# The MLPs of a two-layer decoder step: up and down projections apart, hidden features through DRAM, two token chunks multiplied as 2x2 blocks in seven products (Strassen)

## The chip, the core and the metric

One core of a Trainium2 chip runs the whole program. The metric is the device time of one execution in microseconds (us), lower is better. The engines go by their names in the profile: PE is TensorE's matmul and PEld its weight load, DVE is VectorE, ACT is ScalarE, POOL is GpSimd, and SP issues every DMA of this kernel in one queue, in program order. Each engine runs its own instructions in order and waits on semaphores of the others.

## The reference, cut to what matters

One inference step over 1024 prompt tokens and 8 x 8 sample tokens, 1088 in all, through two layers of width 1024. Layer 0 is a gated mixer, layer 1 a dilated attention; after each of them comes the same kind of MLP, with a hidden width of 4096:

```python
def sq_relu_mlp(x, w_up, w_down):
    h = jnp.square(jax.nn.relu(jnp.einsum('bld,df->blf', x, w_up)))
    return jnp.einsum('blf,fd->bld', h, w_down)
...
xp = layer_norm(ALPHA * xp + mp, ln1_g[layer], ln1_b[layer])
xp = layer_norm(ALPHA * xp + sq_relu_mlp(xp, w_mlp_up[layer], w_mlp_down[layer]), ln2_g[layer], ln2_b[layer])
```

All of it is float32; the new cache rows are outputs too, which for the kernel means 56 copies of up to 1 MB from DRAM to DRAM.

## The kernel before, in words

Activations lie with the features on the 128 partitions and the tokens along a row. `XH` and `XL` hold the layer's input as a high and a low part in float32r (`split`: ACT rounds the high part, DVE or POOL subtracts it), `ACC` holds the sum that is being built up, all three with 8 blocks of 1088 tokens. The tokens are cut into three chunks (`TC`), of 384, 384 and 320 in some order.

A float32 product is three matmuls on float32r parts, high x high, high x low and low x high (`group`), summed in one PSUM bank; there are 8 banks (`ps`). A weight piece (`raw`, 1024 numbers on a partition, two buffers) comes from DRAM on the SP queue and is converted into high and low parts (`convert`: ACT, then POOL) in one of six `wp` buffers. `pump` converts the next piece after a matmul group while fewer than `cap` (6 here) are converted and not released.

`mlp` goes through the hidden width in eight blocks of 512 (`ff`). In a block, `up` makes the 512 hidden features of every chunk: 24 matmuls a group (8 feature blocks x 3), then ACT takes relu from PSUM into `t`, DVE multiplies it onto PSUM, ACT writes the high part into the scratch tile `h` and DVE the low part. `down` multiplies them by the block's rows of the down weights, 12 matmuls a group, and DVE adds the group onto `ACC` from PSUM. Nothing of the hidden features leaves the core. Of the 56 cache copies one is issued (`shift`) after each weight piece of layer 0's MLP.

The order in which work of several streams is emitted comes from a model of the engines (`Model`, `Driver`). All operations pass through a recorder, so that every row of the profile has its line, L188, and rows are told apart by their tiles.

## Time and profile before

| | |
|---|---|
| median of 3 runs | 2763.81 us (2763.4 to 2763.81) |
| span of the profiled execution | 2761.2 us |
| PE busy | 2695.0 us, 98% of the span |
| DVE, ACT, POOL busy | 1058.6, 761.3, 626.8 us |
| moved by the DMA queue SP issues to | 220.20 MB, 25.0% of 16 engines' span |

The span runs from the first to the last instruction of one profiled execution; the times of the runs are 2.2 to 2.6 us longer than this span. A busy share is an average over stages; the two MLPs are two of them, from about 340 to 1105 us and from about 1950 to 2707 us.

### The profile page before, as it was taken

How to read it: one execution, taken by the hardware profiler on the slowest of the kernel's cores; microseconds unless marked ns; L12 is line 12 of the kernel's file. 1: busy time of each engine (PE TensorE's matmuls, PEld its weight loads, DVE VectorE, ACT ScalarE, POOL GpSimd, SP SyncE). 2: the span in 40 equal slices, each digit the busy share in tenths (PEclk: the TensorE clock that was granted, in tenths of full speed). 3: DMA queues.
4: the chain of work that ended last, by engine and by line, in shares of the span. 5: the costliest groups of instructions: out<-in, count | busy, mean ns of one | idle time of the engine just before them, and what ended most of it. 6: DMA issues, size and time to landing. Idle time of an engine off the chain costs nothing.

```text
span 2761.2 us, 42360 instructions
## 1 busy us (share of the span) xinstructions
PE 2695.0 (98%) x17783; PEld 2596.4 (94%) x17783; DVE 1058.6 (38%) x2422; ACT 761.3 (28%) x1531; POOL 626.8 (23%) x357
## 2 busy tenths in 40 slices
PE   9999999999999999899999999998899999999997
PEld 8999999999999999888888888887799999999997
DVE  4306472222222223843434434447922222222226
ACT  4213152221122112432333333333432212211221
POOL 1421243221222222311211211214542112122212
PEclk9999999999999999999999999999999999999999
DMA  4111112333333342033332332331111111111111
GB/s 151 44 52 32 46 39 96 114 117 133 137 137 117 133 156 103 27 100 111 100 116 81 94 113 78 105 97 40 46 54 46 39 46 47 46 40 46 51 35 66
DMA packets 271901, 222.92 MB, mean 81 GB/s; under 512 B 9519, under 2 KB 262651, under 8 KB 270813
## 3 DMA queue, kind: packets, MB, share of 16 engines
q1 hardware_dynamic: 271708, 220.20, 25.0%
q8 instruction: 140, 2.29, 0.3%
q14 instruction: 53, 0.43, 0.0%
HBM read 207.94 MB, written 65.97 MB: 99 GB/s over the span
## 4 chain that ended last, share of the span: by engine, by line
PE 87%; DVE 6%; issue 2%; POOL 1%; ACT 0%; POOLq 0%; DVEq 0%; ACTq 0%
PE ps L188 87%; DVE ACC L188 2%; DVE t L188 1%; DVE h L188 1%; POOL ACC L188 1%; DVE wp L188 1%; DVE XL L188 0%; POOL t L188 0%; ACT t L188 0%; DVE ps L188 0%; POOLq L1529 0%; ACT h L188 0%; POOLq L188 0%; DVEq L188 0%; ACTq L188 0%
## 5 line engine op out<-in xcount | busy, mean ns | idle before, releaser
L188 PE MATMUL ps<-XH,wp 128*128 128x384 f32 (+1 forms) x5952 | 1504.6, 331 | 2.2 <-ACT XH L188 2.2
L188 PEld LDWEIGHTS ps<-XH,wp 128*128 128x128 f32 x5952 | 1058.6, 189 | 14.2 <-issue 9.3
L188 PE MATMUL ps<-XL,wp 128*128 128x384 f32 (+1 forms) x2976 | 974.1, 327 | 3.5 <-DVE XL L188 3.4
L188 POOL TENSOR_TENSOR wp<-raw,wp 128x1024 fp32r<-128x1024 f32 (+1 forms) x196 | 469.2, 2396 | 1737.8 <-ACT wp L188 1687.4
L188 PE MATMUL ps<-h,wp 128*128 128x384 f32 (+1 forms) x4896 | 820.3, 328 | 0.4 <-DVE h L188 0.4
L188 PEld LDWEIGHTS ps<-h,wp 128*128 128x128 f32 x4896 | 812.9, 189 | 2.6 <-DVE h L188 0.8
L188 PEld LDWEIGHTS ps<-XL,wp 128*128 128x128 f32 x2976 | 561.6, 189 | 7.3 <-DVE XL L188 5.5
L188 DVE TENSOR_TENSOR ACC<-ACC,ps 128x384 f32<-128x384 f32 (+4 forms) x369 | 217.7, 595 | 430.5 <-PE ps L188 430.3
L188 ACT ACTIVATE wp<-raw 128x1024 fp32r<-128x1024 f32 (+1 forms) x200 | 206.7, 1036 | 497.5 <-PE ps L188 303.2
L188 ACT ACTIVATE t<-ps 128x384 f32<-128x384 f32 (+4 forms) x280 | 135.2, 485 | 649.9 <-PE ps L188 649.4
L188 DVE TENSOR_TENSOR ps<-t,ps 128x320 f32<-128x320 f32 x168 | 90.8, 541 | 416.1 <-ACT t L188 416.1
L188 ACT ACTIVATE h<-ps 128x384 fp32r<-128x384 f32 (+5 forms) x263 | 123.1, 471 | 273.8 <-PE ps L188 171.9
L188 DVE TENSOR_TENSOR h<-ps,h 128x320 fp32r<-128x320 f32 (+1 forms) x180 | 96.1, 534 | 167.8 <-ACT h L188 91.3
L188 ACT ACTIVATE t<-t,h 128x128 f32<-128x128 f32 (+1 forms) x184 | 80.4, 438 | 130.5 <-DVE h L188 130.3
L188 DVE COPY t<-ps 128x512 f32<-128x512 f32 (+3 forms) x116 | 69.9, 606 | 115.8 <-PE ps L188 110.7
L188 DVE SCALAR_TENSOR_TENSOR ACC<-ACC,ps 128x384 f32<-128x384 f32 (+1 forms) x96 | 50.7, 529 | 138.0 <-PE ps L188 69.7
L188 DVE CUSTOM_DVE_ANT_0 t<-ps,wp 128x128 f32<-128x128 f32 (+1 forms) x184 | 56.6, 345 | 102.7 <-PE ps L188 101.5
L188 PE MATMUL ps<-ident,wp 128*128 128x128 f32 (+1 forms) x480 | 69.7, 269 | 14.0 <-DVE wp L188 10.9
L188 PEld LDWEIGHTS ps<-ident,wp 128*128 128x128 f32 (+1 forms) x480 | 54.1, 141 | 25.3 <-issue 17.1
L188 PE MATMUL ps<-t,h 128*64 128x128 f32 (+1 forms) x1136 | 71.5, 283 | 1.1 <-DVE t L188 1.1
L188 DVE COPY h<-ps 64x128 f32<-64x128 f32 (+4 forms) x85 | 35.4, 423 | 89.6 <-PE ps L188 89.5
L188 PE MATMUL ps<-h,ACC 64*128 64x128 f32 (+1 forms) x384 | 66.2, 472 | 0.0
(122 smaller groups left out, 1479.0 us busy)
## 6 DMA issues: line engine op xcount, KB each, us to landing
raw<-w_mlp_up SPq DMA_DIRECT2D x64, 512.0 KB
raw<-w_mlp_down SPq DMA_DIRECT2D x64, 512.0 KB
wp<-cache_kv_w SPq DMA_DIRECT2D x80, 256.0 KB
raw<-w_qkv_c SPq DMA_DIRECT2D x36, 512.0 KB
wp<-cache_kv_w SPq DMA_DIRECT2D x128, 128.0 KB
kvs<-cache_kv_w SPq DMA_DIRECT2D x16, 992.0 KB
raw<-w_in_ab SPq DMA_DIRECT2D x16, 512.0 KB
t<-x_prompt SPq DMA_DIRECT2D x16, 256.0 KB
```

The source lines that it names most:

```text
L188: r = fn(*a, **k)
```

## The change

The hidden width is no longer worked through block by block. Each MLP now has an up stage and a down stage. Its first 512 hidden features are made as before and put into DRAM as they are (`H0`); at the end they come back for the last part of the down stage. The other 3584 are made in 14 up units (`up_unit`) of 256 and used in 14 down units (`down_unit`), each of 512 hidden features by 512 outputs.

In a unit, the two chunks of 384 tokens (`sa`, `sb_`) and the weights form 2x2 blocks. The usual eight block products become seven, with four sums of weight blocks and four of activation blocks beforehand and seven sums of products behind (the Winograd form of Strassen's scheme). The chunk of 320 tokens (`sc`, `plain`) is multiplied as before. So a unit has 84 matmuls over 384 tokens and 48 over 320, where the same work had 96 and 48.

For that, `convert_unit` takes a raw piece of 2048 numbers a partition (now one DMA of 1 MB) and makes four `wp` pieces from it: two of plain blocks (1024 numbers, ACT and POOL) and two of sums (DVE adds, then ACT and POOL on 2 x 512). The sums of the layer's input (`terms`) are made once, by DVE and ACT, after the layer norm; three go into the `h` tiles, the fourth takes the place of a block in `XH` and `XL`. The sums of hidden features that the down stage needs are made with each up unit (`close`). All nine results of an up unit are split into parts (`split_out`) in places cut out of `ACC` and stored to DRAM (`Ha`, `Hb`, `Hc`, `Ht`); this is put off (`chores`): one such chore is emitted after each product of the next unit. `ACC` itself is stored first (`saved`), and comes back (`reload`) at the turn from up to down, where ACT then applies the residual's factor and offset (`scale`). In the down stage the hidden features of the next 512 are loaded into the free half of `XH` and `XL` and of the `h` tiles (`load`, `load_term`) while those of this half are used. The last up unit of an MLP (`last`) has its products in another order, issues the first loads and reloads between them, and puts out all chores at once.

Besides, `tmp` has 9 buffers for 7, a `fetch` looks at the number of raw pieces that are open, the cache copies are spread over both layers, and the program is built with a smaller DMA scratch area.

```diff
     def mlp_specs(l):
-            s += [('up', UP[l], 512 * ff + 128 * j) for j in range(4)]
+        s = [('up', UP[l], 128 * j) for j in range(4)]
+        s += [('su', UP[l], 0, 512 + 256 * u, j) for u in range(14) for j in range(4)]
+        s += [('sd', DN[l], 512 * ff, 512 * v, j) for ff in range(1, 8) for v in range(2) for j in range(4)]
+        s += [('dn', DN[l], 0, 256 * j) for j in range(4)]
         return s
...
+    def convert_unit(i, j):
+        raw = raws[i - j]
+        k, c = raw.shape[1] // 2, raw.shape[2] // 2
...
+        a11, a12, a21, a22 = raw[:, 0, :, :c], raw[:, 1, :, :c], raw[:, 0, :, c:], raw[:, 1, :, c:]
+        hl = wp_tile([2, 2 * k, c])
+        hi, lo = hl[:, 0], hl[:, 1]
+        if j in (0, 3):
+            h4, l4 = (x.rearrange("p (o k) c -> p o k c", o=2) for x in (hi, lo))
+            split(raw[:, :, :, :c] if j == 0 else raw[:, :, :, c:], h4, l4, pool)
+        else:
+            x, y = (tmp().rearrange("p (k c) -> p k c", k=k) for z in range(2))
+            if j == 1:
+                tt(y, a21, a22, ALU.add)
+                tt(x, y, a11, ALU.subtract)
+            else:
+                tt(x, a21, a11, ALU.subtract)
+                tt(y, a12, a22, ALU.subtract)
+                tt(y, y, x, ALU.subtract)
+            split(x, hi[:, :k], lo[:, :k], pool)
+            split(y, hi[:, k:], lo[:, k:], pool)
+        if j == 3:
+            del raws[i - j]
+        ready[i] = [(hi[:, :k], lo[:, :k]), (hi[:, k:], lo[:, k:])]
...
+    def product(out, w, x, k_n, start=True, stop=True, cs=slice(0, P)):
...
+        pump()
+        if chores:
+            chores.pop(0)()
...
+        places = [flat[:, 768 * i:768 * i + 768] for i in range(11)]
+        late = [flat[:, 8704 - 768 * i:9472 - 768 * i] for i in range(7, 0, -1)]
+        ring = {'all': itertools.cycle(places), 'late': itertools.cycle(late)}
...
+        def terms(b_done):
+            TH.extend(new([3072], F32R, f"h{i}") for i in range(3))
+            t1, t2, t3 = (x.rearrange("p (z k c) -> p z k c", z=2, k=4) for x in TH)
+            for k in range(4):
+                b11, b12, b21, b22 = ACC[:, k, sa], ACC[:, k, sb_], ACC[:, 4 + k, sa], ACC[:, 4 + k, sb_]
+                s1, s2, s3, s4 = (tmp()[:, :n] for z in range(4))
+                tt(s1, b12, b11, ALU.subtract)
+                tt(s2, b22, s1, ALU.subtract)
+                vec.scalar_tensor_tensor(s3, b12, cols[:, bi + k:bi + k + 1], b22, op0=ALU.add, op1=ALU.subtract)
+                tt(s4, b21, s2, ALU.subtract)
+                split(s2, t2[:, 0, k], t2[:, 1, k])
+                split(s1, t1[:, 0, k], t1[:, 1, k])
+                split(s3, t3[:, 0, k], t3[:, 1, k])
+                yield [b_done]
+                split(s4, XH[:, k, sb_], XL[:, k, sb_])
...
+        def reload(r, k):
+            sp.dma_start(ACC[:, r:r + k], saved[:, r:r + k])
+        def scale(k):
+            if k < 4:
+                act(ACC[:, k], ACC[:, k], AF.Identity, scale=ALPHA, bias=ab[:, 8 * l + k:8 * l + k + 1])
+            else:
+                act(ACC[:, k], ACC[:, k], scale=ALPHA)
+        def split_out(g, dst, eng=None):
+            act(g[:, 0].bitcast(F32R), g[:, 1])
+            tt(g[:, 1], g[:, 1], g[:, 0], ALU.subtract, eng)
+            sp.dma_start(dst, g)
...
+        def squared_here(x):
+            vec.scalar_tensor_tensor(x, x, 0.0, x, op0=ALU.max, op1=ALU.mult)
...
+            def plain(i, k):
+                q = bank()[:, :m]
+                yield from product(q, w(i)[0], c1, 4, stop=False)
+                yield from product(q, w(i)[1], c2, 4, start=False)
+                e = place(m, last)
+                squared(e[:, 1], q)
+                chores.append(lambda: split_out(e, Hc[c][:, :, 2 * k + kb], pool))
+            def out(name, x, q):
+                if name == 'b12':
+                    v[name] = tmp()[:, :n]
+                else:
+                    g[name] = place(n, last)
+                    v[name] = g[name][:, 1]
+                tt(v[name], x, q, ALU.add)
+                squared_here(v[name])
+            def took():
+                v['p1'] = tmp()[:, :n]
+                act(v['p1'], Q['1'])
+            def u2():
+                v['u2'] = tmp()[:, :n]
+                tt(v['u2'], v['p1'], Q['6'], ALU.add)
+            def u3():
+                v['u3'] = tmp()[:, :n]
+                tt(v['u3'], v['u2'], Q['7'], ALU.add)
+            def u4():
+                tt(v['u2'], v['u2'], Q['5'], ALU.add)
+            def close():
+                for x in ('t1', 't2', 't3', 't4'):
+                    g[x] = place(n, last)
+                s1, s2, s3, s4 = (g[x][:, 1] for x in ('t1', 't2', 't3', 't4'))
+                def sums():
+                    tt(s1, v['b12'], v['b11'], ALU.subtract)
+                    tt(s2, v['b22'], s1, ALU.subtract)
+                def more_sums():
+                    tt(s3, v['b12'], v['b22'], ALU.subtract)
+                    tt(s4, v['b21'], s2, ALU.subtract)
+                def piece(x, dst, eng=None):
+                    return lambda: split_out(g[x], dst, eng)
+                chores.extend([sums, more_sums, piece('b11', Ha[c][:, :, kb]), piece('t2', Ht[c][1][:, :, kb], pool),
+                               piece('t1', Ht[c][0][:, :, kb]), piece('t3', Ht[c][2][:, :, kb], pool),
+                               piece('b21', Ha[c][:, :, 2 + kb]), piece('b22', Hb[c][:, :, 2 + kb]),
+                               piece('t4', Hb[c][:, :, kb])])
...
+            if last:
+                while chores:
+                    chores.pop(0)()
+                yield from plain(1, 0)
+                yield from plain(4, 1)
+                yield from p('2', 1, 1, b21)
+                reload(0, 3)
+                yield from p('3', 3, 1, b22)
+                load(0, 1)
+                yield from p('1', 1, 0, b11)
+                took()
+                release()
+                yield from p('6', 2, 0, t2v)
+                load_term(0, 1, 1)
+                u2()
+                out('b11', v['p1'], Q['2'])
+                for k in range(3):
+                    scale(k)
+                yield from p('7', 3, 0, t3v)
+                load_term(0, 1, 2)
+                u3()
+                yield from p('5', 2, 1, t1v)
+                load_term(0, 1, 0)
+                release()
+                release()
+                out('b22', v['u3'], Q['5'])
+                u4()
+                out('b12', v['u2'], Q['3'])
+                yield from p('4', 4, 1, t4v)
+                release()
+                out('b21', v['u3'], Q['4'])
+                close()
+                while chores:
+                    chores.pop(0)()
+                reload(3, 1)
+                reload(4, 4)
+                chores.extend([lambda k=k: scale(k) for k in range(3, 8)])
+                return
+            yield from p('1', 1, 0, b11)
+            took()
+            yield from plain(1, 0)
+            yield from p('2', 1, 1, b21)
+            release()
+            out('b11', v['p1'], Q['2'])
+            yield from p('6', 2, 0, t2v)
+            u2()
+            yield from p('7', 3, 0, t3v)
+            u3()
+            yield from p('5', 2, 1, t1v)
+            release()
+            out('b22', v['u3'], Q['5'])
+            u4()
+            yield from p('3', 3, 1, b22)
+            release()
+            out('b12', v['u2'], Q['3'])
+            yield from p('4', 4, 1, t4v)
+            out('b21', v['u3'], Q['4'])
+            yield from plain(4, 1)
+            release()
+            close()
...
+        def load(c, z):
+            for x, d in ((XH, 0), (XL, 1)):
+                sp.dma_start(f(x[:, 4 * z:4 * z + 4, sa]), Ha[c][:, d])
+                sp.dma_start(f(x[:, 4 * z:4 * z + 4, sc]), Hc[c][:, d])
+            for x, d in ((XH, 0), (XL, 1)):
+                sp.dma_start(f(x[:, 4 * z:4 * z + 4, sb_]), Hb[c][:, d])
+        def load_term(c, z, i):
+            sp.dma_start(f(parts(z)[i]), Ht[c][i])
...
+                q1 = yield from p(1, 0, b11)
+                p1 = tmp()[:, :n]
+                act(p1, q1)
+                yield from plain(1, j1)
+                q2 = yield from p(1, 1, b21)
+                done()
+                onto(j1, sa, q2)
+                onto(j1, sa, p1, pool)
+                q6 = yield from p(2, 0, t2v)
+                u2 = tmp()[:, :n]
+                tt(u2, p1, q6, ALU.add)
+                q7 = yield from p(3, 0, t3v)
+                u3 = tmp()[:, :n]
+                tt(u3, u2, q7, ALU.add)
+                q5 = yield from p(2, 1, t1v)
+                done()
+                onto(j2, sb_, q5)
+                onto(j2, sb_, u3, pool)
+                tt(u2, u2, q5, ALU.add)
+                q3 = yield from p(3, 1, b22)
+                done()
+                onto(j1, sb_, q3)
+                onto(j1, sb_, u2, pool)
+                q4 = yield from p(4, 1, t4v)
+                onto(j2, sa, q4)
+                onto(j2, sa, u3, pool)
+                yield from plain(4, j2)
...
+        w4 = [weight() for j in range(4)]
+        b_done = Flag()
+        sums_in = drv.spawn(terms(b_done), [lns[t] for t in order])
+        for t in order:
+            c0, w_ = TC[t]
+            yield [lns[t]]
+            sp.dma_start(saved[:, :, c0:c0 + w_], ACC[:, :, c0:c0 + w_])
+            for j in range(4):
+                q = yield from up_group(w4[j], t)
+                r = tmp()[:, :w_]
+                squared(r, q)
+                sp.dma_start(H0[:, j, c0:c0 + w_], r)
+                if t == order[-1]:
+                    release()
+            if t == tb:
+                b_done.done = True
+        yield [sums_in]
+        for u in range(14):
+            yield from up_unit(u, u == 13)
+            if u % 2:
+                shift()
+        for c in range(7):
+            z = 1 - c % 2
+            if c < 6:
+                load(c + 1, 1 - z)
+                for i in range(3):
+                    load_term(c + 1, 1 - z, i)
             else:
+                r = 4 - 4 * z
+                sp.dma_start(f(XL[:, r:r + 4]), H0)
+                chores.extend([lambda: None] * 9)
+                for s in (sc, sb_, sa):
+                    for k in (r, r + 2):
+                        chores.append(lambda x=XH[:, k:k + 2, s], y=XL[:, k:k + 2, s]: split(f(y), x, y))
+            for v in range(2):
+                yield from down_unit(v, z)
+                if v:
+                    shift()
+            while chores:
+                chores.pop(0)()
+        w4 = [weight() for j in range(4)]
+        if not first:
+            finish_rows()
+        for t in order:
+            k3, k7 = Flag(), Flag()
+            if not first:
+                drv.spawn(finish(t, k3, k7, order[-1]))
+            for j in range(4):
+                yield from down(w4[j], j, t, 0, first)
```

What the change does to the instruction streams shows at two places.

The first is DVE in the up stage. Before, these are DVE's rows for three groups of an up block (`ps` is a PSUM bank, `t` a scratch tile, `h` the hidden features):

```order
L188 TENSOR_TENSOR ps598_6964<-t599_6989,ps598_6964 128x320
L188 TENSOR_TENSOR h2268_3181<-ps598_6964,h2268_3181 128x320
L188 TENSOR_TENSOR ps600_6994<-t603_7024,ps600_6994 128x384
L188 TENSOR_TENSOR h1282_3323<-ps600_6994,h1282_3323 128x384
L188 TENSOR_TENSOR ps604_7029<-t605_7054,ps604_7029 128x384
```

Now these stand in the middle of one up unit (`raw` is the next unit's weight piece, `ACC` the places cut out of it, `t` a scratch tile):

```order
L188 TENSOR_TENSOR ACC7_160<-t503_5530,ps508_5572 128x384
L188 SCALAR_TENSOR_TENSOR ACC7_160<-ACC7_160 128x384
L188 TENSOR_TENSOR t510_5606<-t503_5530,ps509_5590 128x384
L188 TENSOR_TENSOR t513_5622<-raw477_5251 128x512
L188 TENSOR_TENSOR t514_5623<-raw477_5251 128x512
L188 TENSOR_TENSOR t514_5623<-t514_5623,t513_5622 128x512
L188 TENSOR_TENSOR ACC7_160<-ACC7_160 128x384
L188 TENSOR_TENSOR t515_5634<-t510_5606,ps511_5608 128x384
L188 TENSOR_TENSOR ACC7_160<-t515_5634,ps516_5636 128x384
```

Each row of before reads a PSUM bank; now a whole unit has 25 rows of DVE, of which 7 read a PSUM bank and 18 read SBUF alone.

The second place is the turn from the last up unit to the first down unit of layer 0. It does not exist before: in layer 0's MLP, SP's queue held weight fetches and cache copies only, as in

```order
L188 DMA raw370_4334<-w_mlp_up 128x8x128
L188 DMA kvs0<-cache_kv_w128 16x7680
L188 DMA raw377_4402<-w_mlp_up 128x8x128
L188 DMA kvs1<-cache_kv_w512 16x16384
L188 DMA raw385_4492<-w_mlp_down 128x4x256
```

Now SP has the nine stores of the last unit but one, the reload of `ACC`'s first three blocks, five loads of stored features into `XH` and `XL`, and then these (`h1289`, `h2290`, `h0288` are the `h` tiles, `hb00` and `ht001` stored features of the first 512 of the down stage, `ha06` and so on those that the last unit makes):

```order
L188 DMA XL6_159<-hb00_73 128x4x384
L188 DMA h1289_3517<-ht001_88 128x1536
L188 DMA h2290_3518<-ht002_89 128x1536
L188 DMA h0288_3516<-ht000_87 128x1536
L188 DMA ha06_72<-ACC7_160 256x1x384
L188 DMA ht061_106<-ACC7_160 256x1x384
L188 DMA ht060_105<-ACC7_160 256x1x384
L188 DMA ht062_107<-ACC7_160 256x1x384
L188 DMA ha06_72<-ACC7_160 256x1x384
L188 DMA hb06_79<-ACC7_160 256x1x384 x2
L188 DMA ACC7_160<-saved0_108 128x1088
L188 DMA ACC7_160<-saved0_108 128x4352
```

and ACT, at the same place, has these (`ab4` holds the residual's offsets, so a row with 1088 numbers is `scale`; `t634` and `t650` take the first product of the down unit's two halves out of PSUM):

```order
L188 ACTIVATE ACC7_160<-ACC7_160 128x384 x7
L188 ACTIVATE wp632_6882<-raw587_6348 128x1024
L188 ACTIVATE ACC7_160<-ACC7_160,ab4_157 128x1088
L188 ACTIVATE t634_6888<-ps631_6875 128x384
L188 ACTIVATE wp636_6897<-raw609_6568 128x1024
L188 ACTIVATE ACC7_160<-ACC7_160 128x1088
L188 ACTIVATE wp637_6907<-t638_6908 128x512
L188 ACTIVATE wp637_6907<-t639_6909 128x512
L188 ACTIVATE ACC7_160<-ACC7_160 128x1088 x3
L188 ACTIVATE t650_6996<-ps649_6989 128x384
```

So the copies of both halves' first products stand behind `scale` on ACT, `scale` behind the two last reloads on SP, and these behind the stores of the last unit.

## Rows read from the trace of the kernel before

**Rows 1.** The page's first part: busy us, share of the span, instructions.

```profile
PE 2695.0 (98%) x17783; PEld 2596.4 (94%) x17783; DVE 1058.6 (38%) x2422; ACT 761.3 (28%) x1531; POOL 626.8 (23%) x357
```

**Rows 2.** Chain that ended last, the MLPs' pieces: start us, us, what.

```profile
377.84 727.02 PE ps L188 x4404
...
1995.92 711.38 PE ps L188 x4316
```

**Rows 3.** Timeline of PE at a change of chunks: start us, us.

```profile
1042.86 0.31 PE L188 MATMUL ps<-XL,wp 128*128 128x320 f32 x1
...
1043.74 0.31 PE L188 MATMUL ps<-XL,wp 128*128 128x320 f32 x1
...
1045.28 0.33 PE L188 MATMUL ps<-XL,wp 128*128 128x384 f32 x1
...
1049.96 0.33 PE L188 MATMUL ps<-XL,wp 128*128 128x384 f32 x1
```

**Rows 4.** Busy time by stretch, both MLPs: length, engines, PEclk, DMA share, GB/s.

```profile
600.00:1000.00 400.00, 400.00 (x2431) 400.00 (x2430) 108.16 (x204) 82.92 (x138) 81.55 (x34) 1.00 0.37 134
2100.00:2600.00 500.00, 500.00 (x3037) 500.00 (x3036) 135.38 (x254) 104.62 (x174) 103.15 (x43) 1.00 0.15 45
```

**Rows 5.** Groups by shape, POOL: count, busy us, mean ns of one, idle before.

```profile
L188 POOL TENSOR_TENSOR wp<-raw,wp 128x1024 fp32r<-128x1024 f32 x192 | 463.8, 2418 | 1712.5 <-ACT wp L188 1662.1 <-DMA wp<-cache_kv_w 23.1 <-PE ps L188 15.8
...
L188 POOL TENSOR_TENSOR h<-h,t 128x384 f32<-128x384 f32 x8 | 7.9, 1007 | 5.4 <-DVE t L188 5.4
L188 POOL TENSOR_TENSOR ACC<-ACC,t 128x384 f32<-128x384 f32 x6 | 7.2, 1204 | 17.2 <-ACT t L188 17.2
...
L188 POOL TENSOR_TENSOR h<-h,t 128x320 f32<-128x320 f32 x4 | 3.5, 870 | 0.0
...
L188 POOL TENSOR_TENSOR h<-h,t 128x512 f32<-128x512 f32 x2 | 2.6, 1296 | 24.9 <-DVE h L188 24.9
```

**Rows 6.** Groups by shape, DVE.

```profile
L188 DVE TENSOR_TENSOR ACC<-ACC,ps 128x384 f32<-128x384 f32 x218 | 120.1, 553 | 306.1 <-PE ps L188 306.1
...
L188 DVE TENSOR_TENSOR t<-t,ACC 128x384 f32<-128x384 f32 x36 | 29.7, 824 | 0.9
...
L188 DVE TENSOR_TENSOR h<-h,t 128x512 f32<-128x512 f32 x14 | 9.7, 692 | 3.3 <-POOL h L188 2.9
```

**Rows 7.** Timeline of DVE in the layer norm ahead of layer 1's MLP.

```profile
1963.78 0.54 DVE L188 SCALAR_TENSOR_TENSOR ACC<-ACC,ps 128x384 f32<-128x384 f32 x1
...
1969.04 2.13 DVE L188 TENSOR_TENSOR t<-t,ACC 128x384 f32<-128x384 f32 x1
1971.10 0.54 DVE L188 SCALAR_TENSOR_TENSOR ACC<-ACC,ps 128x384 f32<-128x384 f32 x1
1971.67 0.56 DVE L188 TENSOR_TENSOR t<-t,ACC 128x384 f32<-128x384 f32 x1
```

**Rows 8.** Timeline of POOL in the same stretch.

```profile
1960.80 5.27 POOL L188 TENSOR_TENSOR wp<-raw,wp 128x1024 fp32r<-128x1024 f32 x2 [3.67 <-ACT wp L188]
...
1968.00 2.76 POOL L188 TENSOR_TENSOR wp<-raw,wp 128x1024 fp32r<-128x1024 f32 x1 [1.93 <-ACT wp L188]
```

**Rows 9.** Busy time by stretch, at the program's start, where many transfers are open.

```profile
2.00:12.00 10.00, 5.90 (x29) 4.90 (x30) 3.51 (x5) 4.55 (x9) 1.95 (x2) 1.00 0.97 308
12.00:22.00 10.00, 9.99 (x86) 9.79 (x85) 5.92 (x10) 7.08 (x14) 0.85 (x1) 1.00 0.98 326
1.80:24.70 22.90, 18.59 (x135) 17.39 (x136) 11.32 (x17) 13.24 (x24) 2.80 (x2) 1.00 0.91 296
```

**Rows 10.** The DMA queue's own waits: us in total, times, longest.

```profile
SPq L1529 <- DMA y_s<-t: 1.8, 1, 1.8
```

**Rows 11.** Groups by shape, ACT: a conversion's high part.

```profile
L188 ACT ACTIVATE wp<-raw 128x1024 fp32r<-128x1024 f32 x192 | 201.9, 1053 | 496.3 <-PE ps L188 303.2 <-issue 152.3 <-DMA raw<-w_in_ab 16.8
```

**Rows 12.** Busy time by stretch: an idle PE in the layer norm, then TensorE's clock.

```profile
1964.40:1968.80 4.40, 0.21 (x2) 0.14 (x1) 4.33 (x5) 1.06 (x1) 2.47 (x2) 0.95 0.68 229
1968.80:1971.80 3.00, 3.00 (x8) 2.10 (x8) 2.93 (x4) 1.11 (x2) 1.96 (x1) 0.50 0.05 16
```

More of the change, by code (lines that the diff above doesn't have):

```diff
@@ L836, in down @@
-        def down(w, j, t, first, last=False):
-            c0, n = TC[t]
+        H0, Ha, Hb, Hc, Ht, saved = hidden[l]
+        tc_, tb, ta = order
+        sa, sb_, sc = (slice(TC[t][0], TC[t][0] + TC[t][1]) for t in (ta, tb, tc_))
+        n, m = TC[ta][1], TC[tc_][1]
+        TH = []
+        flat = ACC.rearrange("p k c -> p (k c)")
+        places = [flat[:, 768 * i:768 * i + 768] for i in range(11)]
+        late = [flat[:, 8704 - 768 * i:9472 - 768 * i] for i in range(7, 0, -1)]
+        ring = {'all': itertools.cycle(places), 'late': itertools.cycle(late)}
@@ new lines, in place, with rows @@
+        def place(w, last):
+            return next(ring['late' if last else 'all'])[:, :2 * w].rearrange("p (z c) -> p z c", z=2)
+        def rows(r, k, s):
+            return XH[:, r:r + k, s], XL[:, r:r + k, s]
+        def terms(b_done):
[13 more added lines that the diff above has]
+                split(s4, XH[:, k, sb_], XL[:, k, sb_])
```

187 lines of the change are left out of this document (109 added, 78 removed).

## The prediction

> **What bounds the kernel now.** I read the page's first part, then the chain of waits, then TensorE row by row. PE is busy for 2695.0 of 2761.2 us, and no other engine for more than 38% [rows 1]. The chain says where that is so without a gap: from 377.84 us it stays on PE for 727.02 us, from 1995.92 us for 711.38 us [rows 2]. These two pieces are the MLPs after their layer norms. So whatever shortens PE there is gained, as long as no other engine falls behind. The price of one matmul is the distance of starts, not its shown duration, since matmuls overlap. Every third matmul is one on the low part: nine such distances over 384 tokens run from 1045.28 to 1049.96, so 27 matmuls take 4.68 us, 173.3 ns each; over 320 tokens six take 0.88 us, 146.7 ns each [rows 3]. A mix of two to one gives 164.4 ns, and 400 us of the MLP hold 2431 of them, 164.5 ns each [rows 4]: nothing but matmuls bounds this stretch. DVE is busy there for 27%, ACT 21%, POOL 20%, and the DMA engines are moving for 37% at most.
>
> **The products.** A unit had 96 x 173.3 + 48 x 146.7 ns = 23.7 us and now has 84 x 173.3 + 48 x 146.7 = 21.6 us. There are 28 units a layer, 56 in all: 672 matmuls fewer, 672 x 173.3 ns = 116.5 us. This is the whole gain; each part below is a cost against it.
>
> **Up units: DVE and POOL.** By count of the code, DVE has in a unit 7 operations with one input in PSUM (0.55 us), 13 over 384 numbers from SBUF alone (0.56 when undisturbed) and 5 over 512 (0.69): 3.9 + 7.3 + 3.5 = 14.7 us [rows 6, 7]. POOL has two conversions of 1024 (2.4), four of 512 (1.3), two pieces of 384 (1.0) and two of 320 (0.87): 13.7 us [rows 5]. Each alone fits into 21.6. They don't run freely side by side, though. A sum from SBUF alone that takes 0.56 us at 1971.67 took 2.13 at 1969.04, while POOL converted from 1968.00 to 1970.76: DVE came to its end 0.4 us behind POOL's [rows 7, 8]. One with an input in PSUM took its usual 0.54 at 1963.78 in the middle of POOL's conversions. And POOL's two conversions from 1960.80 took 5.27 us for 4.8, so an operation of DVE that is let in between two of POOL costs POOL about 0.25. Bounds for a unit: if all ten of POOL's operations have one of DVE's let in behind them (2.5) and the other eight run while POOL is idle (3 x 0.56 + 5 x 0.69 = 5.1), POOL and these need 13.7 + 2.5 + 5.1 = 21.3 us, just under PE's 21.6. If none is let in cheaply, it is 18 operations (10.8) + 13.7 = 24.5. Between these ends I take 22.4, near the low one: eight PSUM banks let PE run most of a unit ahead of DVE, conversions are ahead of PE by about a unit, and the blocked operations in rows 7 are those of a DVE that was already the last. Cost: 28 x 0.8 = +22 us; ends 0 and 28 x 2.9 = +81.
>
> The Trainium skill, page SBUF — State Buffer, section "Who interferes with whom", states this as a rule that speaks against the change: a DVE instruction with two SBUF inputs and a GpSimd instruction that reads SBUF take turns on a shared read port, each for its whole length. The rows agree (DVE blocked until POOL's end); by the bare rule an up unit would take the 24.5 us.
>
> **Down units.** DVE: 18 operations from PSUM and 5 over 512, 13.4 us. POOL: the same conversions (10.0) and eight sums onto `ACC`, 1.01 to 1.20 us each [rows 5]: 18.1 to 19.6, with five operations of DVE let in some 1.3 more. That is 90% of 21.6. PE waits for POOL only through weights, which are a unit ahead. Taken +5 us over 28 units; ends 0 and +19 (22.3 us a unit).
>
> **Transfers.** An up unit stores 3.4 MB, fetches 1.05 and has half a cache copy of 1 MB; a down unit loads 3.0. With many transfers open the queue moved 308 and 326 GB/s [rows 9], I take 316. Then a unit's 5 MB need 16 us of 21.6, beside PE. It costs nothing while units follow each other; it has no cover at the turn. SP's fetch of a weight piece waits for POOL's last conversion of an older one, and two stores stand behind it whose places ACT wants for the unit's last relu; ACT may lose some 4 us a unit there (a 1 MB fetch ahead of the store and a landing). It has room: two conversions of 1024 (1.05), four of 512 (half of that, with its start 0.6) and 14 smaller ones at about 0.5 are 11.5 us of 21.6 [rows 11]. The cache copies that move into other stages delay a fetch behind them by 3.2 us each (1 MB), where a piece is fetched two ahead and lasts 72 matmuls, 11.8 us: nothing.
>
> **The turn from up to down.** Count from the last up unit's start; PE would end it at 21.6 and the first down unit at 43.2. The queue first has the 3.4 MB of the unit before, from about 1 to 12 us, landed by 14 (a landing took 1.8 us [rows 10]). Then come 1.67 MB of `ACC` (to 19) and the first unit's features. Its first product needs the first three of nine loads, 2.23 MB, to 26, landed at 28; its seventh kind of product waits for the last of 6.03 MB, at 40. Next the last unit's seven pieces, 2.75 MB, to 47, landed at 49; then one block of `ACC` (0.56 MB, landed at 53) and four more (2.23 MB, landed at 60). On ACT, `scale` for these blocks stands ahead of the copies that empty the first bank of each half; five take 1.1 us each, from the 1.05 of a conversion of like size [rows 11]. So the first half's copy comes at 54, the second's at 65. A half uses nine banks, there are eight, so PE stops at the end of each half until that copy is made, and ends the unit at about 68 for 43.2: 25 us. After an idle PE of about 4 us the granted clock stood at 0.50, 1.2 GHz, in the next 3.0 us [rows 12]: 2 us more. Together 27 us a layer, +54. Ends: 14 a layer if the reloads land before the copies are due (bytes from the first reload on, no landings), 34 if the queue moves 296 GB/s (the whole start's rate [rows 9]) and the pieces are late by a few us.
>
> **The start of an MLP.** `terms` adds 32 operations from SBUF to DVE behind the layer norm, 32 x 0.56 = 18 us, with some three POOL conversions 25. PE has 96 matmuls of the last chunk (16.6 us) and the first three products of the first unit (24 x 173.3 and 24 x 146.7 ns, 7.7 us), 24 us in all, before it needs the last sums of `terms`. +3 us a layer, +6; ends 0 and +16. The tail behind the MLP of layer 1 and the layer norms keep their order: no cost.
>
> **The sum.** −116.5 + 22 + 5 + 54 + 6 = −29.5 us on the profiled 2761.2, whose runs take 2.6 more at the median: 2763.8 − 29.5 = 2734 us.
>
> **The rivals.** (a) *The shared port sets the up stage*: a unit of 24.5 us, +81 for +22, gives 2793. From 23.4 us a unit on the gain is gone: 28 x 1.84 = 51.5 us above PE's own time, with the 65 of the other costs, are the 116.5. For it: rows 7 and 8, and that the two ends are only 3 us apart, on either side of PE's 21.6. Against it: the operations come spread over the unit, and a POOL that is ahead by a unit blocks DVE less. (b) *The turn is cheap* (14 us a layer) and the up units go at PE's pace: −116.5 + 28 + 5 + 6, 2686 us. For it: the loads are issued as early as their places allow, and the queue is the only thing that sets them. Against it: the last reloads stand behind the last unit's stores. (c) *POOL sets the down stage*: 22.3 us a unit, +14 more than taken, 2748; rows 5 put it at the very edge. (d) *Transfers set the stages*: 5 MB at 231 GB/s are PE's 21.6 us, at 210 they are 23.8, which over 56 units is +123 and ends well above 2785; the rates of rows 9 speak against it.
>
> **How the numbers follow.** Forecast 0.50 (2705 to 2760), (b) 0.23, (a) 0.17, (c) 0.06, (d) 0.04. The range, 2680 to 2785, takes in (b), (c) and the lower part of (a). A measurement of this kernel tells 0.2% (5.5 us) from no change. Slower by more: (a) and half of (d), 0.18, with a little of the forecast's end; same: 0.05; faster: 0.76.
>
> **What would show it.** Right: PE has 672 matmuls over 384 tokens fewer at the same distances; at each turn PE is idle in several pieces with DMA and then ACT's `scale` named, about 25 us a layer, and half the clock for a few us behind it; in the up stage DVE is busy for over 85% with operations on `ACC` alone at a mean near 1 us for 0.56 undisturbed. Wrong: PE waits for DVE or for `wp` in every up unit, 2 us or more each (a); no gap over 5 us at the turn (b); gaps in the down units with POOL named (c).

## The result

The changed kernel takes 2846.0 us (median, 2839.6 to 2852.9), the one before 2763.8: 3.0% slower, ratio 1.0298 with an interval from 1.0277 to 1.0319. The forecast was 2734, the range 2680 to 2785, so the result is outside it and on the other side. The profiled execution has a span of 2849.5 us for 2761.2, 88.3 more.

The first part of its page, to set beside [rows 1] (busy us, share of the span, instructions):

```profile
span 2849.5 us, 43940 instructions
...
PE 2644.4 (93%) x17111; PEld 2529.3 (89%) x17111; DVE 1678.5 (59%) x3171; ACT 933.8 (33%) x1878; POOL 1288.4 (45%) x893
```

TensorE now stands idle or at half its clock for parts of both MLPs. The next view is busy time by stretch in the first layer's MLP, to set beside [rows 4]: three up units, ten more, the last up unit, two down units, twelve more.

```profile
core 0: us, PE busy (x) PEld busy (x) DVE busy (x) ACT busy (x) POOL busy (x), PEclk, DMA share, GB/s
424.30:489.10 64.80, 64.80 (x397) 64.80 (x396) 54.39 (x65) 29.91 (x58) 42.86 (x26) 1.00 0.45 153
489.10:754.10 265.00, 233.22 (x1322) 229.73 (x1321) 187.82 (x247) 99.21 (x199) 151.13 (x100) 0.94 0.54 186
754.10:796.00 41.90, 24.80 (x134) 23.63 (x133) 30.05 (x45) 16.27 (x31) 18.17 (x13) 0.82 0.71 255
796.00:867.20 71.20, 52.30 (x265) 50.47 (x266) 33.58 (x50) 22.67 (x34) 40.07 (x30) 0.82 0.79 296
867.20:1130.30 263.10, 261.17 (x1586) 259.95 (x1585) 173.30 (x277) 66.48 (x99) 223.55 (x166) 1.00 0.57 210
```

A unit is 132 matmuls, 21.6 us at PE's pace. The first three up units take that (64.8), and the last twelve down units almost (263.1 for 259.2). The ten up units between take 265 us for 216: PE is idle for 31.8 of them, and its mean granted clock is 0.94. The last up unit and the first two down units take 113.1 us for 64.8. Over both layers the up units ahead of the last cost 98 us more than their matmuls, the turn (last up unit and two down units) 100, the other down units 6: 204, and 204 − 116.5 is the 88 that the span has grown.

**The up units.** What PE waits for from 489 to 754, in a list of waits (us in total, times, longest):

```profile
PE ps L188 <- ACT ACC L188: 31.5, 9, 5.4
```

and what ACT itself waits for in the same stretch:

```profile
ACT ACC L188 <- DMA hb<-ACC: 117.3, 9, 14.8
ACT wp L188 <- DVE t L188: 36.0, 19, 3.3
```

Nine times, once a unit, ACT stands still for 13 us until a store to `hb` has landed. One such unit, first SP's issues, then ACT, then PE (start, us, what; in brackets the idle time before and what ended it):

```profile
631.06 0.56 SPq L188 DMA_DIRECT2D raw<-w_mlp_up  x1
632.07 2.04 SPq L188 DMA_DIRECT2D hb<-ACC  x2
```

```profile
639.33 0.44 ACT L188 ACTIVATE ACC<-ps 128x320 f32<-128x320 f32 x1 [13.09 <-DMA hb<-ACC]
639.80 0.97 ACT L188 ACTIVATE ACC<-ACC 128x320 f32<-128x320 f32 x2
640.68 0.47 ACT L188 ACTIVATE t<-ps 128x384 f32<-128x384 f32 x1
641.05 1.14 ACT L188 ACTIVATE wp<-t 128x512 fp32r<-128x512 f32 x2
642.09 0.43 ACT L188 ACTIVATE ACC<-ps 128x320 f32<-128x320 f32 x1
```

```profile
635.82 0.34 PE L188 MATMUL ps<-XH,wp 128*128 128x384 f32 x1
639.82 0.45 PE L188 MATMUL ps<-XH,wp 128*128 128x384 f32 x1 [3.66 <-ACT ACC L188]
```

The operation at 639.33 is the relu that ends a unit (`squared` in the second `plain`). It writes into a place of the ring of eleven that `ACC` is cut into; a unit uses nine, so this place held `b22` of the unit before. `b22` is the sixth of the seven pieces that `close` lists, and is stored at the ninth of the next unit's eleven products. At 632.07 its store is issued behind a fetch of 1 MB, and lands 7.2 us later. PE goes on 0.05 us after the relu has emptied its bank. Behind the relu on ACT stand the copy of the next unit's first product (640.68), two conversions and the next relu, so PE has used up its eight banks. The chain of waits goes round in 27.1 us, and the store is a link of it:

```profile
604.89 7.21 DMA hb<-ACC
...
612.21 0.45 ACT ACC L188
...
625.32 2.42 DVE ACC L188
...
628.27 2.08 issue
630.35 0.55 DVE t L188
...
631.50 0.57 DVE ACC L188 x2
632.07 7.16 DMA hb<-ACC
...
639.33 0.45 ACT ACC L188
...
659.20 7.18 DMA hb<-ACC
...
666.49 0.45 ACT ACC L188
```

From ACT's late operations the chain passes over DVE's sums to the low parts of `b21` (from 628.13 to 630.42) and, behind two more operations, of `b22` (631.50), behind which SP issues `b22`'s store: late store, late ACT, late DVE, late store. The turns of DVE and POOL are in it too: the square at 625.32 and the low part of `b21` take 2.42 and 2.29 us for 0.56, while POOL converts from 624.92 to 630.01.

**The turn.** Waits of PE and of ACT from 754 to 868:

```profile
PE ps L188 <- ACT t L188: 13.9, 2, 8.9
PE ps L188 <- DMA XH<-ha: 12.7, 1, 12.7
PE ps L188 <- DMA XL<-ha: 3.2, 1, 3.2
PE ps L188 <- POOL wp L188: 3.0, 1, 3.0
```

```profile
ACT ACC L188 <- DMA ACC<-saved: 31.2, 3, 20.2
...
ACT wp L188 <- DMA raw<-w_mlp_down: 12.0, 1, 12.0
ACT ACC L188 <- DMA hb<-ACC: 11.5, 2, 9.9
```

The 8.9 us wait is one of the two that the forecast described: `scale(3)` stands ahead of the copy of the first half's first product, and PE needs that copy's bank for the half's last product (ACT, then PE):

```profile
822.30 1.20 ACT L188 ACTIVATE ACC<-ACC,ab 128x1088 f32<-128x1088 f32 x1 [20.15 <-DMA ACC<-saved]
823.41 0.47 ACT L188 ACTIVATE t<-ps 128x384 f32<-128x384 f32 x1
```

```profile
823.93 0.63 PE L188 MATMUL ps<-XH,wp 128*128 128x320 f32 x1 [8.87 <-ACT t L188]
```

The second, at the end of the second half, did not come: its copy was made at 832.49, in time. The 12.7 us are the wait for the first features, which the forecast had at some 6 us: the first block of `ACC` and the first loads were issued 33 us into the last up unit, where the forecast had the queue reach them at 14 and 19. The second of the `ACT t` waits (5.0 us, in the second down unit) is not in the forecast: ACT stood in a conversion whose weights the queue held behind the nine loads of the next pair, 6.8 MB.

### The profile page after: what moved, and what is told of

It is laid out like the page before. It is cut to its first block, busy times and chain, and to the rows that moved or that the text cites. A ratio compares the mean times of both kernels' runs of the same rounds, so it can differ in the third digit from the quotient of the medians.

```text
span 2849.5 us, 43940 instructions
## 1 busy us (share of the span) xinstructions
PE 2644.4 (93%) x17111; PEld 2529.3 (89%) x17111; DVE 1678.5 (59%) x3171; ACT 933.8 (33%) x1878; POOL 1288.4 (45%) x893
## 3 DMA queue, kind: packets, MB, share of 16 engines
q1 hardware_dynamic: 357596, 437.80, 45.2%
## 4 chain that ended last, share of the span: by engine, by line
PE 48%; DVE 13%; DMA 9%; issue 7%; ACT 3%; POOL 2%; SPq 1%; ACTq 0%; DVEq 0%; POOLq 0%
PE ps L188 48%; DVE ACC L188 7%; DMA hb<-ACC 6%; DVE t L188 4%; ACT ACC L188 2%; SPq L188 1%; DMA raw<-w_mlp_down 1%; ACT wp L188 1%; DMA h<-ht 1%; DVE wp L188 1%; DVE h L188 1%; POOL ACC L188 1%; DMA XL<-h 1%; ACT t L188 0%; DVE XL L188 0%
## 5 line engine op out<-in xcount | busy, mean ns | idle before, releaser
L188 PE MATMUL ps<-XH,wp 128*128 128x384 f32 (+1 forms) x7232 | 1856.5, 334 | 135.4 <-ACT ACC L188 66.1
L188 PEld LDWEIGHTS ps<-XH,wp 128*128 128x128 f32 x7232 | 1310.8, 193 | 159.8 <-ACT ACC L188 98.6
L188 PE MATMUL ps<-XL,wp 128*128 128x384 f32 (+1 forms) x3616 | 1197.1, 331 | 8.9 <-DMA XL<-ha 6.3
L188 PE MATMUL ps<-h,wp 128*128 128x384 f32 (+1 forms) x2304 | 423.0, 339 | 5.1 <-DVE ACC L188 2.1
L188 PEld LDWEIGHTS ps<-h,wp 128*128 128x128 f32 x2304 | 405.6, 191 | 9.4 <-DVE t L188 4.0
L188 POOL TENSOR_TENSOR wp<-t,wp 128x512 fp32r<-128x512 f32 x224 | 312.0, 1414 | 175.2 <-ACT wp L188 166.6
L188 DVE TENSOR_TENSOR ACC<-ACC 128x384 f32<-128x384 f32 (+1 forms) x200 | 208.5, 1049 | 178.8 <-ACT ACC L188 177.5
L188 POOL TENSOR_TENSOR ACC<-ACC,t 128x384 f32<-128x384 f32 (+1 forms) x233 | 244.3, 1071 | 58.2 <-DVE ACC L188 43.1
L188 POOL TENSOR_TENSOR ACC<-ACC 128x320 f32<-128x320 f32 (+2 forms) x124 | 146.7, 1185 | 266.2 <-ACT ACC L188 225.1
L188 DVE TENSOR_TENSOR t<-t,ps 128x384 f32<-128x384 f32 x280 | 153.1, 547 | 70.3 <-ACT t L188 45.5
```

Source lines behind the costliest of these rows:

```text
L188: r = fn(*a, **k)
```

## Experiments

Lengths in us, layer 0 / layer 1, from the distances of the units' first matmuls (so a wait ahead of a unit's first matmul counts to the unit before it):

| kernel | time | up units 0 to 12 | last up | down 0 | down 1 | down 2 |
|---|---|---|---|---|---|---|
| at PE's pace | | 280.8 | 21.6 | 21.6 | 21.6 | 21.6 |
| changed | 2846.0 | 329.9 / 329.9 | 41.9 / 45.2 | 42.8 / 43.4 | 28.3 / 28.2 | 21.7 / 21.7 |
| e1, b22 second | 2762.2 | 285.6 / 284.1 | 42.3 / 43.1 | 43.2 / 43.6 | 28.1 / 29.8 | 21.7 / 21.7 |
| e2, no low parts on POOL | 2764.7 | 292.4 / 288.7 | 39.5 / 40.5 | 42.6 / 44.2 | 29.9 / 27.9 | 21.7 / 21.7 |
| e3, no copies in the up stage | 2838.6 | 332.5 / 325.8 | 41.1 / 39.4 | 43.7 / 43.5 | 25.4 / 24.3 | 21.7 / 21.7 |
| e4, scalings late | 2848.6 | 339.6 / 324.9 | 40.9 / 40.5 | 32.7 / 32.6 | 39.5 / 41.7 | 21.7 / 21.7 |
| e6, e1 and e4, second loads later | 2723.1 | 283.6 / 285.4 | 43.5 / 41.7 | 31.4 / 32.3 | 21.7 / 21.8 | 21.7 / 21.7 |
| e7, loads ahead of the stores | 2720.7 | 283.3 / 285.7 | 31.4 / 30.3 | 34.1 / 34.7 | 24.1 / 22.5 | 29.1 / 28.5 |
| e8, e6 with squares on ACT | 2824.6 | 329.2 / 328.2 | 48.9 / 48.8 | 31.7 / 33.7 | 21.7 / 21.7 | 21.7 / 21.7 |
| e11, e6 without POOL's low parts | 2690.8 | 281.3 / 281.3 | 29.1 / 29.4 | 31.4 / 33.4 | 21.7 / 21.7 | 21.7 / 21.7 |
| e12, e6 with copies moved | 2724.1 | 284.6 / 285.8 | 43.1 / 41.6 | 31.9 / 32.7 | 21.7 / 21.7 | 21.7 / 21.7 |
| e13, e7 tuned | 2720.9 | 283.6 / 284.0 | 32.1 / 31.7 | 33.9 / 34.7 | 21.7 / 21.7 | 29.6 / 28.2 |

### The order of the stores, the shared port, or the bytes

**e1.** One piece changes its place in a list:

```diff
-chores.extend([sums, more_sums, piece('b11', ..), piece('t2', ..), piece('t1', ..), piece('t3', ..), piece('b21', ..), piece('b22', ..), piece('t4', ..)])
+chores.extend([sums, more_sums, piece('b11', ..), piece('b22', ..), piece('t2', ..), piece('t1', ..), piece('t3', ..), piece('b21', ..), piece('t4', ..)])
```

> The changed kernel with one piece of the up unit, b22, stored second instead of sixth; nothing else moves. Theory 'place': in the up units ACT's last relu waits for the store of b22, whose place it reuses; that store stands behind a 1 MB fetch and takes 7.2 us. Stored four products earlier it has long landed, ACT never stops, and units 3 to 12 of a layer take 21.6 to 22.5 us instead of 22 to 30: 2745 to 2770 us. Rival 'port': DVE and POOL, which take turns, set the unit; the wait on the store only fills time in which DVE is late anyway: units of 24.5 us or more remain, at least 2795 us. Rival 'queue': all transfers are late because the queue holds too many bytes, whatever their order: about 2840.

2762.2 us, 0.9995 of the kernel before (0.9986 to 1.0004): the whole loss of 84 us is gone, and the kernel is level with the one before. (Four other pieces are stored one product later than they were.) Of the first layer's up units ahead of the last, twelve take 21.6 us and one 25.9. ACT waits for no store there; its list from 427 to 713 has this at its head, and PE's has one wait over 0.2 us:

```profile
ACT wp L188 <- DVE t L188: 147.5, 37, 7.4
```

```profile
PE ps L188 <- DVE ACC L188: 1.9, 1, 1.9
```

DVE and POOL do take turns: on DVE the mean of a `t<-t` of 384 numbers, 0.56 us undisturbed, is 2.49 here, and POOL's first conversions of successive units start 22.7 us apart (DVE by shape; POOL's timeline; busy time over one such period):

```profile
L188 DVE TENSOR_TENSOR ACC<-ACC 128x384 f32<-128x384 f32 x25 | 31.2, 1257 | 4.4 <-ACT ACC L188 4.3
L188 DVE SCALAR_TENSOR_TENSOR t<-t 128x384 f32<-128x384 f32 x4 | 10.0, 2494 | 0.1
```

```profile
583.78 5.07 POOL L188 TENSOR_TENSOR wp<-raw,wp 128x1024 fp32r<-128x1024 f32 x2
...
606.44 5.06 POOL L188 TENSOR_TENSOR wp<-raw,wp 128x1024 fp32r<-128x1024 f32 x2
...
629.12 5.05 POOL L188 TENSOR_TENSOR wp<-raw,wp 128x1024 fp32r<-128x1024 f32 x2
```

```profile
606.44:629.12 22.68, 22.68 (x140) 22.68 (x139) 21.27 (x26) 10.04 (x22) 15.79 (x11) 1.00 0.73 242
```

DVE is busy for 21.3 of these 22.7 us, POOL for 15.8: DVE, held up by POOL, sets the period. So the pair needs 22.7 us where PE needs 21.6, falls behind by 1.1 us a unit, and in the first layer PE feels nothing of it for eleven units.

**e2.** The other side of the same loop: the weights' low parts in the up units leave POOL, so DVE is free of it. The low part is not subtracted here.

```diff
-tt(lo, src, f(hi), ALU.subtract, pool)
+act(lo, src)
```

> The changed kernel, but in the up units the low parts of the converted weights are written by ACT as a plain copy of the weight instead of by POOL as the difference (so the low part is not subtracted: that part of the computation is left out). POOL loses 10 of its 13.7 us a unit, ACT gains 4.6. Theory 'port': with POOL's conversions gone, operations of DVE on ACC alone take 0.56 us each instead of 1.03 in the mean, and the gaps in the up units vanish: 2745 to 2770. Theory 'place': the order of the stores is as it was, so the wait of ACT on b22's store remains, shortened only by what DVE brings that store forward: gaps of 1 to 3 us a unit remain, 2780 to 2830.

2764.7 (one run), where the expectation had it by the port and not by the place. DVE's sums on `ACC` alone take 0.56 us for 1.09 in the changed kernel. Gaps of 1.1 to 3.3 us remain in the last up units, but the first eight units of each layer take 21.6. So both theories hold a part: either link cut, the loop opens. The late place without POOL's conversions costs 8 to 12 us a layer, the port without the late place 3 to 5 ahead of the last unit (e1), the two together 49. This edit takes away POOL's own work along with the turns, and doesn't tell these two apart.

**e3.** The copies that the up stage issues are left out.

```diff
-    shift()
+    next(copies)
```

> The changed kernel without the seven cache copies of 1 MB that each up stage issues (these 14 copies are left out altogether). Theory 'place': each copy is issued behind the two stores of hb, so it is not in their way; units 3 to 12 stay at 25 to 29 us and the time above 2830. Rival 'queue': the bytes in the queue make the stores late; every second unit loses its gap, about 5 us each, 12 of them: about 2790.

2838.6 (one run); units 5 to 12 stay at 27 to 30 us in the first layer and 24 to 30 in the second. It isn't the bytes of these copies; and in e1 the same bytes as in the changed kernel go beside units at PE's pace.

### The turn

**e4.** The five scalings go from the first five products behind the turn to those ahead of their sums:

```diff
-chores.extend([lambda k=k: scale(k) for k in range(3, 8)])
+due = {17: 3, 21: 4, 24: 6, 28: 5, 31: 7}
+chores.extend([lambda k=due.get(i): k and scale(k) for i in range(1, 32)])
```

> The changed kernel with the scalings of the five last blocks behind the turn moved from the first products of each half to where the sums need them (block 3 at product 17, blocks 4 to 7 at products 21 to 31 of the first two down units). Theory of the prediction: ACT's scale stands ahead of the copy that empties the second half's first bank, so the 8.7 us gap in the first down unit goes, with its half clock: 8 to 14 us a layer, 2822 to 2834. Rival: the loads themselves are late, the gap only moves to a later product: within 5 us of 2846.

By the rows above the gap in question ends the first half, not the second. 2848.6 (ratio 1.0295, 1.0270 to 1.0319): no gain. The first down unit takes 10 to 11 us less, as expected; the second takes 11 to 14 more. ACT's waits from 804 to 880:

```profile
ACT wp L188 <- DMA raw<-w_mlp_down: 22.6, 1, 22.6
```

The stall in `scale` had hidden one behind it: a conversion on ACT, ahead of the next copy that PE needs, waits for weights, and their fetch stands on the queue behind nine loads that are needed only a pair of units later.

**e6.** So these loads too go to a later product (with e1 and e4):

```diff
+chores[10] = second_load     # load(1, 0) and its three terms
-            if c < 6:
+            if 0 < c < 6:
```

> b22 stored second, the five scalings late, and in addition the nine loads of the second pair of down units issued half a unit into the first down unit instead of ahead of it. Theory: the 15 to 17 us gap that late scalings alone bring into the second down unit is ACT waiting, in a conversion that stands ahead of the copy PE needs, for a weight fetch that the queue holds behind these 6 MB; with the fetch ahead of them the gap goes. First down unit 33 us for 43, second about 22 for 28: some 16 us a layer less than with b22 second alone, 2725 to 2735. Rival: the queue has the same bytes to move and SP is held by the reloads anyway, so the gap moves again: 2750 or more.

2723.1, 0.9853 of the kernel before (0.9838 to 0.9868): the second down unit is at 21.7 and the first at 31 to 32.

**e7.** The last up unit no longer flushes what is left of the unit before, and the first pair's loads go ahead of the last stores:

```diff
-                while chores:
-                    chores.pop(0)()
...
                 yield from p('2', 1, 1, b21)
-                reload(0, 3)
+                load_own(0, 1)
```

> As the kernel with the loads of the second pair half a unit later, and in addition the last up unit no longer makes ready and stores all that is left of the unit before it ahead of its own products: those pieces go one per product, the loads for the first down unit are issued as soon as the products that read the old rows are done, ahead of the last pieces' stores, the blocks of ACC come back one by one in the order in which the sums need them, and the last unit's pieces get places that nothing needs soon (free places of ACC and the half of the h tiles that is read last). Theory: the turn is late because the loads stand behind stores in SP's order, 33 us into the last unit where the rows are free after 11; last up unit about 22 to 26 us for 42, first down unit 25 to 32: 2680 to 2700. Rival: the bytes themselves (about 12 MB between the last up unit's start and the second down unit) set the turn: not under 2715.

2720.7, 0.9850 (0.9834 to 0.9867): level with e6, and not under the 2715 that the rival 'bytes' allows. The last up unit gains 11 to 12 us; down units 0 to 2 give 10 to 13 back.

**e12.** Two copies of 1 MB leave each turn of e6 for the middle of the down stage:

```diff
-            if u % 2:
+            if u % 2 and u < 13:
                 shift()
...
-                if v:
+                if v and c or c in (3, 4):
```

> b22 second, scalings late, second loads half a unit later, and the two cache copies of 1 MB at each turn moved to the middle of the down stage; the squares stay on DVE. Theory 'bytes': the queue is full from the last up unit to the third down unit, 2 MB less are 3 to 6 us a layer: 2711 to 2717. Rival 'order': what PE waits for stands ahead of these copies: within 3 us of 2723.

2724.1: nothing, so the bytes of these copies don't set the turn.

**e13.** e7 with the same, `scale(0)` behind the first copy, and the second pair's loads ahead of the last pieces:

```diff
-                scale(0)
+plan = {.., 2: lambda: scale(0), ..}
-todo = [..] + own[1:] + [second_load]
+todo = [..] + [lambda: load(1, 0)] + own[1:] + [..]
```

> The kernel that issues the loads of the first down unit ahead of the last stores, with the copies out of the turn, block 0 of ACC scaled behind the copy of the first product, and the second loads ahead of the last pieces' stores; the squares stay on DVE. Theory: of what the last up unit gained there (12 us a layer) the third down unit then no longer gives back its 7 us, and the first one loses less: 2697 to 2708. Rival 'bytes': the queue is full either way, 2714 or more.

2720.9: the second down unit is at PE's pace, the third still takes 28 to 30 us. The time lies where the rival 'bytes' has it, as e7's does, but neither theory is shown: without the copies nothing changes, and with the loads earlier the third unit waits as before. What sets the 31 us a layer that this turn still costs is settled only in part (e11, below, takes 11 to 14 of e6's 31 to 32 away). The bytes of the loads and reloads themselves stay a rival that no run here tests: from 740 to 770 us of e6, around the turn, the DMA engines are busy throughout (share 1.00, 369 GB/s).

### What is left of the port

**e8.** Relu and square of the four sums of a unit leave DVE, to take load off the pair:

```diff
-                squared_here(v[name])
+                squared(v[name], v[name])
```

> b22 second, scalings late, second loads half a unit later, and in addition relu and square of the four sums of an up unit as two operations of ACT in place of one of DVE. Theory: with b22 stored early DVE and POOL, which take turns, still need 22.7 us a unit for PE's 21.6; PE's lead hides this for some eleven units, then come gaps of about 2 us in unit 11 and 4 and 4 us at the start of the last. Without these four operations on DVE (0.56 to 2.5 us each) the pair needs under 21.6 and these gaps go: some 10 us a layer with the clock, 2698 to 2708. Rival: ACT stands in order and waits for each of DVE's sums, the pair's period stays at 22.7 and the gaps with it: 2718 or more.

2824.6, 1.0227 of the kernel before (1.0213 to 1.0241): over 100 us worse than e6, and neither theory had it. Each of DVE's sums now has two ACT operations behind it, and ACT's next conversion, for which POOL waits, stands behind those. The three engines wait for one another in turn:

```profile
604.70 2.37 POOL L188 TENSOR_TENSOR wp<-raw,wp 128x1024 fp32r<-128x1024 f32 x1 [0.96 <-ACT wp L188]
...
605.00 2.48 DVE L188 TENSOR_TENSOR ACC<-ACC 128x384 f32<-128x384 f32 x1 [2.77 <-ACT ACC L188]
...
607.41 0.54 DVE L188 TENSOR_TENSOR ACC<-t,ps 128x384 f32<-128x384 f32 x1
...
607.98 1.08 ACT L188 ACTIVATE ACC<-ACC 128x384 f32<-128x384 f32 x2 [3.02 <-DVE ACC L188]
...
608.97 1.04 ACT L188 ACTIVATE wp<-raw 128x1024 fp32r<-128x1024 f32 x1
...
610.14 2.38 POOL L188 TENSOR_TENSOR wp<-raw,wp 128x1024 fp32r<-128x1024 f32 x1 [3.07 <-ACT wp L188]
```

DVE's sum at 607.41 stands behind the operation at 605.00, which had to wait out POOL's conversion (to 607.07); ACT's squares wait for the sum, ACT's conversion for the squares, POOL for the conversion: 27.3 us a unit from unit 5 on. Two more kernels carried this edit, and show the same up units. One has e12's copies moved as well (2824.9 us), the other is e13 with it (2824.7):

> As the kernel with the squares on ACT, and the two cache copies of 1 MB that each turn issues moved to the middle of the down stage. Theory 'bytes': from the last up unit to the third down unit the queue moves at its full rate, 300 to 410 GB/s, so 2 MB less are 5 to 6 us a layer less: 10 us under the kernel with the squares on ACT. Rival 'order': the first down unit waits for loads that stand ahead of these copies anyway: within 4 us of it.

> The kernel that issues the loads ahead, with squares on ACT, copies out of the turn, block 0 of ACC scaled behind the copy of the first product, and the second loads ahead of the last pieces' stores. Theory 'bytes': the turn then starts some 8 us earlier and has 2 MB less to move, 20 us a layer less than without these: 2675 to 2690. Rival 'order': what the loads gain ahead the third down unit gives back, as before: within 6 us of the kernel with the copies moved.

**e11.** e2's edit on top of e6, again with the low part not subtracted:

> b22 second, scalings late, second loads half a unit later, and the low parts of the up units' weights written by ACT as a plain copy instead of by POOL as a difference (the subtraction of the low part is left out). Theory: the gaps of 2 us in unit 11 and of 4 and 4 at the start of the last up unit, which remain with b22 second, come from DVE and POOL needing 22.7 us a unit for PE's 21.6 while they take turns; with POOL's conversions gone they vanish: about 10 us a layer, 2698 to 2708. Rival: they come from the change to the down weights or from the order of the last unit, and stay: 2716 or more.

2690.8, 0.9737 (0.9723 to 0.9750), more than expected. All up units ahead of the last take 21.6 us, and the last 29 for 42 to 43. Busy time by stretch (the up units ahead of the last, the last, two down units):

```profile
425.30:706.60 281.30, 281.30 (x1718) 281.30 (x1717) 193.84 (x324) 190.65 (x347) 53.13 (x50) 1.00 0.64 219
706.60:735.70 29.10, 21.82 (x135) 21.53 (x133) 18.21 (x32) 10.86 (x21) 8.07 (x8) 0.93 0.79 286
735.70:788.70 53.00, 47.17 (x264) 45.85 (x265) 33.34 (x50) 21.57 (x33) 40.05 (x30) 0.91 1.00 375
```

PE has one wait in the last up unit, for the first features (its list of waits from 700 to 736 us):

```profile
PE ps L188 <- DMA XH<-ha: 7.3, 1, 7.3
```

In e6 it is 10.4 us there, behind 4.2 and 3.6 us early in the unit, where PE waits for ACT's and POOL's converted weights. The first reload and the first loads, which stand behind all stores of the unit before, are issued 20 us into the last up unit in e11 (726.33) and 34 in e6 (741.39). So what DVE and POOL fall behind, 1.1 us a unit, is paid at the turn: 2723.1 − 2690.8 = 32 us. As in e2, POOL's own work goes with the turns; that DVE and not POOL is busy all the time (e1) speaks for the turns.

## Why the prediction was wrong

**The products: right.** 17111 matmuls for 17783 are the 672 fewer, and every unit that waits for nothing takes 21.6 us.

**The step that failed: "It costs nothing while units follow each other", under Transfers.** The wait was named there, two stores behind a fetch "whose places ACT wants for the unit's last relu", and priced as a loss of 4 us of ACT's time, which it has to spare. But ACT works in order. Behind that relu stand the copies that empty PE's banks and the operations that DVE waits for, and DVE's lateness comes back as a later store. The wait was 13 us in nine units of the first layer, and the units took 27 us for 21.6. e1, which stores that piece earlier, removes 84 us: +84 in place of 0. It costs this much because DVE and POOL are late as well: without POOL's conversions (e2) the same wait costs 8 to 12 us a layer.

**Up units, DVE and POOL: the period right, the place wrong.** Forecast 22.4 us a unit, between 21.3 and 24.5; the pair runs at 22.7 once nothing else stops it. The forecast let PE pay this in each unit, 28 x 0.8 = 22 us. e11 shows 32 us, 27 of it in the two last up units. By the Trainium skill's bare rule (page SBUF — State Buffer, section "Who interferes with whom": the two take turns, each for the whole length) a unit was to take 24.5; the trace of e1 agrees with the turns and gives 22.7. Operations with an input in PSUM, which pass in 0.54 us, are in neither sum and don't explain the difference; part of it is that DVE's operations are let in between two of POOL's, as the forecast's lower bound assumes (one ends at 609.25, the conversion ahead of it at 608.84, and the next conversion takes 2.71 us for 2.40). Rival (a), the port setting the up stage at 2793, names one link of the loop and is wrong as the whole cause: e1 has the same port and no such loss.

**The turn: 100 us for 54.** The gap behind `scale(3)` came as described, 8.9 us, the one at the end of the second half did not. One term was mis-sized: the 3.4 MB of the unit before were taken as gone after 12 us by their bytes. Their stores wait one by one for low parts from DVE and POOL (SP waits 23 us for the two from 754 to 787), and the first load was issued at 33 us. The nine loads are also 6.8 MB by the sizes in the trace, where the working has 6.03. One term was missed: ACT's conversion for the third down unit waits behind the second pair's loads: 5 us a layer, 15 to 17 in e4. The order of scalings and loads alone is worth 39 us (e6 against e1).

**Down units and the start of the MLP: near in size, in part by luck.** +5 was forecast for the down units, +6 measured. But eleven of the twelve units behind the turn are within 0.3 us of PE's pace in each layer, and 4 of the 6 us lie in the last unit (24.4 and 22.5 us), where PE waits 1.4 us for POOL's weights in the first layer and 0.6 in the second. For `terms` +6 was forecast; the terms above leave about 1 us for all else, and no run takes `terms` apart.

So −116.5 + 98 + 100 + 6 is the measured +88, where −116.5 + 22 + 54 + 5 + 6 was forecast. Rival (d), that the queue's bytes set the stages, falls with e1, whose up units move the same bytes at PE's pace, and with the down units at 21.7 us; at the turn alone bytes stay possible.

The change itself pays: e6, which differs by one list's order, five later scalings and nine later loads, is 1.5% faster than the kernel before.

## What to carry over

When a buffer ring is recycled, write down for each reuse which product frees it and which one wants it, and store in the order of reuse; here a ring of eleven places for nine pieces a unit cost 84 us through one piece that was stored late, beside two engines that were late already. A wait on an engine with time to spare is priced by what stands behind it in that engine's order, not by the engine's busy share. And if a stall is removed, look at once for the one behind it (e4), and if load is moved to another engine, for the loop that the new dependence closes (e8).

## What the runs showed that was not expected

- In the first layer an engine pair 1.1 us a unit slower than PE cost PE nothing for eleven units, 2.3 us in the twelfth, and then 14 us in the last: the last up unit takes 43.5 us in e6 and 29.1 in e11.
- In the changed kernel's first up stage PE has eight gaps of 1.8 to 5.4 us, and behind each of them its granted clock fell to 0.50, 1.2 GHz: 31.8 us of idle time cost another 17 by the clock. In e8's first layer 36 us of idle time in the same thirteen units, in pieces of 0.4 to 2.0 us, went by at a granted clock of 1.00 throughout.
